# Moving work between engines in a bidirectional RWKV-7 and neighbourhood-attention layer: full-height scores, a transposed inverse, a plain state update

## The chip, the cores and the metric

One core of one Trainium2 chip runs the whole layer in one launch. The metric is device time in microseconds (us), the median of three runs. Engines are named as the profile names them: PE (TensorE matmul) with PEld (its weight loads), DVE (VectorE), ACT (ScalarE), POOL (GpSimd) and SP (SyncE, which issues the DMAs).

## The reference, cut to what matters

The layer normalises 2,560 tokens (2,048 of a prompt, 512 of a sample) of width 1,024, projects them, and runs two groups of heads: 2-D neighbourhood attention, and RWKV-7 in both directions. The change touches the second. Its heart is a recurrence over the tokens, for 8 heads of 64 by 64 states and two directions:

```
def rwkv7_step(S, inp):
    r_t, w_t, k_t, v_t, kk_t, kka_t = inp
    s_kk = jnp.einsum('zbhvk,zbhk->zbhv', S, kk_t)
    S = S * w_t[..., None, :] - s_kk[..., :, None] * kka_t[..., None, :] + v_t[..., :, None] * k_t[..., None, :]
    return S, jnp.einsum('zbhvk,zbhk->zbhv', S, r_t)
```

Around it stand a centred shift of the projected columns, a low-rank product for the decay (`w_up`) and one for the rate (`a_up`), a norm of `kk` for each head, and after it a norm of each head, a bonus and a gate. Both groups of heads then meet in an output projection.

## The kernel before, in words

**Jobs.** The recurrence is done in chunks of 64 tokens. A job is a pair of heads (128 channels), a direction and a block of 512 tokens, so eight chunks. Twenty steps n, each with one job forwards and one backwards, make up the stage: `prep(n+2)`, `inverse(n+1)` and the chain of chunks of step n are written down side by side, with the projection of later heads (`feed`, L921) and, towards the end, the output projection (L1400) beside them.

**`prep`** makes the decays (two low-rank products of two matmuls each, L1124, L1125, L1128, L1129), scales queries and keys with them, and forms for each chunk and head the scores between `A` (128 channels, keys) and `QR` (128 channels, queries): L1172. The two heads lie in channels 0 to 63 and 64 to 127, so each of these products contracts over 64 rows of the array, one head in the upper half, one in the lower. L1175 masks the result into `SC`, L1180 transposes `A`.

**`inverse`** inverts the unit triangular 64 by 64 matrix of each chunk: its 32 by 32 diagonal blocks (32 for each direction, one in each partition) by substitution on DVE, 30 rounds of a product (L1211) and a sum (L1213), and the block beside them by small matmuls (L1232, L1236). The blocks come from `SC` through DRAM (`ad`) and go back through DRAM (`td`).

**`chain_chunk`** is the serial part. For each chunk: a product with the state (L1265) and with the values (L1268), an ACT copy (L1272), a product with the inverse (L1275), an ACT copy (L1276), the outputs (L1279, copied out by L1301) and the state's gain (L1283), and on DVE for each head a new state (state + gain) times the decay, written to another buffer (L1295). The next chunk's L1265 of that direction needs it. The array runs these products as 128 rows by 64 columns, L1265 as 128 by 128.

**What sets the order.** A planner (`Plan.run`) takes all operations with their dependencies, gives each a cost from a formula, and writes out one fixed order for each engine, by the longest tail of work behind an operation; for PE it also weighs the form of the array (128 by 128, 128 by 64, 64 by 128, 32 by 32) against the last one. Buffers are rings of fixed places (`memory`): an operation that takes a place waits for the readers of its last owner. On the chip each engine runs its list in that order, and an instruction that isn't ready holds up all behind it. Instructions of ACT and DVE on one PSUM bank are kept apart by waits too.

## Time and profile before

| | us |
|---|---|
| median of three runs | 2608.29 |
| lowest, highest | 2605.26, 2626.35 |
| the profiled execution | 2613.05 |
| its span (first to last instruction) | 2611.3 |

Of the span PE is busy 91%, DVE 69%, ACT 44%, POOL 36%. PE's mean granted clock is 0.938 of full speed. Busy time of PE counts from an instruction's start to its modelled end, and a busy PE can still be one that waits between instructions. The stage that the change touches lies between about 880 us (first scores) and 2550 us (last chunk); ahead of it come the projections and the attention, behind it the last of the output projection.

### The profile page before, as it was taken

What the parts mean: (1) busy time and instruction counts of PE and PEld (TensorE: products, weight loads), DVE (VectorE), ACT (ScalarE), POOL (GpSimd) and SP (SyncE); (2) the same over time, 40 slices, a digit from 0 to 9 for tenths busy, and PEclk for the clock granted to TensorE, in tenths of its full rate; (3) what the DMA queues carried; (4) which work ended last, traced back from release to release, by engine and by line L of the source; (5) the groups of instructions that cost most, each with busy time, mean ns of one, the idle gap of its engine ahead of it and who ended that gap; (6) DMA issues with size and microseconds to landing.
All of it is one profiled execution on the core that took longest, in us unless ns stands there. A gap on an engine that the chain in (4) does not pass through costs nothing. (4 is left out here: it accounts for less than half of the span.)

```text
span 2611.3 us, 54063 instructions
## 1 busy us (share of the span) xinstructions
PE 2374.5 (91%) x20106; PEld 1667.4 (64%) x20106; DVE 1806.3 (69%) x4932; ACT 1147.2 (44%) x2708; POOL 947.3 (36%) x1079
## 2 busy tenths in 40 slices
PE   6999998988879999989999999998999888999996
PEld 5988997766545555555555665555565666676674
DVE  8873563357656477686887858887778876877435
ACT  7632444466655443444444434444445433433321
POOL 2462662011112453345454434554444433430100
PEclk9999999998889999889999869999899888989998
DMA  7344124277765654355454345454444555445556
GB/s 261 136 150 122 64 66 142 90 212 197 226 184 157 193 160 129 91 152 158 127 141 119 118 124 140 126 168 133 120 135 120 150 155 163 139 132 157 162 172 229
DMA packets 323640, 386.21 MB, mean 148 GB/s; under 512 B 132400, under 2 KB 197808, under 8 KB 321200
## 3 DMA queue, kind: packets, MB, share of 16 engines
q1 hardware_dynamic: 323376, 382.74, 49.3%
q8 instruction: 159, 2.61, 0.4%
q14 instruction: 105, 0.86, 0.1%
HBM read 261.36 MB, written 121.27 MB: 147 GB/s over the span
## 5 line engine op out<-in xcount | busy, mean ns | idle before, releaser
L921 PE MATMUL b<-sbuf 128*128 128x512 f16 x2040 | 578.1, 396 | 19.8 <-DMA sbuf<-xd 13.9
L819 PE MATMUL b<-sbuf 128*128 128x256 f16 x3840 | 454.9, 275 | 15.1 <-ACT sbuf L839 9.1
L819 PEld LDWEIGHTS <-sbuf 128*128 128x128 f16 x3840 | 372.9, 99 | 64.0 <-issue 13.4
L1400 PE MATMUL b<-sbuf 128*128 128x512 f32 x960 | 289.1, 433 | 23.8 <-DVE sbuf L1409 14.3
L921 PEld LDWEIGHTS <-sbuf 128*128 128x128 f16 x2040 | 182.8, 100 | 195.3 <-issue 35.2
L1295 DVE CUSTOM_DVE_ANT_0 sbuf<-b,sbuf 64x64 f32<-64x64 f32 x568 | 160.3, 283 | 167.3 <-ACT sbuf L1301 86.9
L1213 DVE TENSOR_TENSOR sbuf<-sbuf 64x30 f32<-64x30 f32 (+2 forms) x600 | 261.5, 436 | 12.3 <-POOL sbuf L1214 2.5
L1211 DVE TENSOR_TENSOR sbuf<-sbuf 64x30 f32<-64x30 f32 (+2 forms) x600 | 251.7, 420 | 9.9
L1400 PEld LDWEIGHTS b<-sbuf 128*128 128x128 f32 x960 | 179.1, 200 | 71.4 <-DVE sbuf L1409 15.6
L1265 PE MATMUL b<-sbuf 128*128 128x128 f32 x608 | 147.2, 328 | 60.7 <-DVE sbuf L1295 51.4
L1265 PEld LDWEIGHTS b<-sbuf 128*128 128x128 f32 x608 | 103.1, 204 | 126.0 <-issue 41.6
L1272 ACT COPY sbuf<-b 64x128 f32<-64x128 f32 x320 | 81.0, 257 | 215.5 <-PE b L1268 194.5
L1301 ACT COPY sbuf<-b 64x128 f32<-64x128 f32 x320 | 82.7, 262 | 186.5 <-PE b L1283 110.9
L1172 PE MATMUL b<-sbuf 64*128 64x128 f32 x1280 | 156.8, 301 | 4.5 <-POOL sbuf L1162 2.2
L1279 PE MATMUL b<-sbuf 128*64 128x64 f32 x1280 | 151.3, 243 | 6.2 <-ACT sbuf L1276 5.9
L1275 PEld LDWEIGHTS b<-sbuf 128*64 128x64 f32 x1280 | 103.5, 143 | 82.4 <-ACT sbuf L1272 34.4
L1175 DVE TENSOR_TENSOR sbuf<-b,sbuf 128x512 f32<-128x512 f32 x160 | 108.0, 685 | 69.0 <-PE b L1172 46.0
L1279 PEld LDWEIGHTS b<-sbuf 128*64 128x64 f32 x1280 | 105.7, 144 | 77.0 <-ACT sbuf L1276 35.9
L1283 PE MATMUL b<-sbuf 128*64 128x64 f32 x1280 | 154.9, 241 | 0.0
L1017 DVE CUSTOM_DVE_ANT_0 sbuf<-b,sbuf 128x384 f32<-128x384 f32 (+2 forms) x160 | 90.2, 578 | 87.8 <-DMA sbuf<-in_b_top_dram 27.7
L1268 PE MATMUL b<-sbuf 128*64 128x64 f32 x1280 | 150.7, 243 | 0.0
L1275 PE MATMUL b<-sbuf 128*64 128x64 f32 x1280 | 145.6, 240 | 4.6 <-ACT sbuf L1272 4.4
(203 smaller groups left out, 4746.2 us busy)
## 6 DMA issues: line engine op xcount, KB each, us to landing
sbuf<-xd SPq DMA_DIRECT2D x60, 512.0 KB
sbuf<-zrk SPq DMA_DIRECT2D x80, 256.0 KB
sbuf<-zl SPq DMA_DIRECT2D x80, 256.0 KB
sbuf<-in_b_mid_dram SPq DMA_DIRECT2D x32, 512.0 KB
sbuf<-mix SPq DMA_DIRECT2D x28, 448.0 KB
sbuf<-in_x_dram SPq DMA_DIRECT2D x20, 512.0 KB
xd<-sbuf SPq DMA_DIRECT2D x10, 1024.0 KB
sbuf<-qtd SPq DMA_DIRECT2D x40, 256.0 KB
```

The lines of the kernel that those rows point to most:

```text
L819: T.matmul(pa, xx[b][:, k, j * 128:(j + 1) * 128], wt[:, k], start=n == 0, stop=n == 23)
L921: T.matmul(pa, W[wt][:, k], xx[k], start=n == 0, stop=n == 23)
L1172: T.matmul(pa[:, u * 128:(u + 1) * 128], both(A[l0:l0 + 64, u]), both(QR[l0:l0 + 64, u]), start=True, stop=True)
L1211: V.tensor_tensor(out=prod, in0=bc(X[:, i + 1:32, i:i + 1], n, i), in1=bc(X[:, i:i + 1, 0:i], n, i), op=ALU.mult)
L1213: V.tensor_tensor(out=X[:, i + 1:32, 0:i], in0=X[:, i + 1:32, 0:i], in1=prod, op=ALU.add)
L1265: T.matmul(pz[:, 0:128], QR[:, c % 4].rearrange("p a s -> p (a s)"), S0, start=True, stop=False)
L1268: T.matmul(pz[0:64, l0:l0 + 64], SC[:, c % 4, h, 0:64], UV[:, c % 4, l0:l0 + 64], start=S0 is None, stop=S0 is None or h == 1)
L1275: T.matmul(pu[0:64, l0:l0 + 64], SC[:, c % 4, h, 0:64], zs[:, l0:l0 + 64], start=True, stop=True)
L1279: T.matmul(pz[64:128, l0:l0 + 64], SC[:, c % 4, h, 64:128], UV[:, c % 4, l0:l0 + 64], start=S0 is None, stop=S0 is None or h == 1)
L1283: T.matmul(pu[l0:l0 + 64, 128:192], AT[:, c % 4, l0:l0 + 64], UV[:, c % 4, l0:l0 + 64], start=True, stop=True)
L1295: V.tensor_tensor_reduce(out=S1[l, q], in0=src, in1=S0[l, q], scale=gt[l, gcol:gcol + 1], scalar=0.0, op0=ALU.add, op1=ALU.max, accum_out= ...
L1400: T.matmul(pa, m, w, start=j == 0, stop=j == len(todo) - 1)
```

## The change

Four things are changed, in `prep`, `inverse`, `chain_chunk` and one line of `shifted`; the planner and its costs stay.

```diff
@@ prep: scores and the low-rank products over all 128 rows
+    qrz = [tile([128, 4, 128], F32, tag="qrz", name=f"qrz{h}") for h in range(2)]
+    for t in qrz:
+        G.memset(t, 0.0)
...
+            V.tensor_tensor(out=ul[64:128], in0=u[64:128], in1=u[64:128], op=ALU.subtract)
...
-        T.matmul(pw, ul[0:64, 0], lw[0][0:64], start=True, stop=False)
+        T.matmul(pw, ul[:, 0], lw[0], start=True, stop=False)
...
-        T.matmul(pb, ul[0:64, 1], lw[1][0:64], start=True, stop=False)
+        T.matmul(pb, ul[:, 1], lw[1], start=True, stop=False)
...
-        V.tensor_scalar(out=s2[:, :, 1:65], in0=s2[:, :, 1:65], scalar1=1.0, scalar2=None, op0=ALU.add)
+        S.activation(out=s2[:, :, 1:65], in_=s2[:, :, 1:65], func=AF.Copy, bias=1.0)
...
+            for h in range(2):
+                S.copy(out=qrz[h][64 * h:64 * h + 64], in_=QR[64 * h:64 * h + 64].rearrange("p c a s -> p c (a s)"))
             for u in range(4):
-                for l0, pa in zip((0, 64), pas):
-                    T.matmul(pa[:, u * 128:(u + 1) * 128], both(A[l0:l0 + 64, u]), both(QR[l0:l0 + 64, u]),
-                             start=True, stop=True)
+                for z, pa in zip(qrz, pas):
+                    T.matmul(pa[:, u * 128:(u + 1) * 128], both(A[:, u]), z[:, u], start=True, stop=True)
@@ shifted
-                V.tensor_copy(dst[:, :, ::-1] if d else dst, pq[0:2].rearrange("p (c s) -> p c s", s=64))
+                S.copy(out=dst[:, :, ::-1] if d else dst, in_=pq[0:2].rearrange("p (c s) -> p c s", s=64))
@@ inverse
-        X, mt = X[0:64], X[64:128]
-        D.dma_start(mt.rearrange("p s t -> p (s t)"), ad)
+        M, X = X[0:64], X[64:128]
+        D.dma_start(M.rearrange("p s t -> p (s t)"), ad)
...
-        V.reciprocal(rm, rm)
-        V.tensor_copy(rs, rm)
-        V.tensor_scalar(out=rm, in0=rm, scalar1=-1.0, scalar2=None, op0=ALU.mult)
+        V.reciprocal(rs, rm)
+        V.tensor_scalar(out=rm, in0=rs, scalar1=-1.0, scalar2=None, op0=ALU.mult)
...
-        V.tensor_tensor(out=X, in0=mt.rearrange("p s t -> p t s"), in1=bc(rm[:, :, None], 32, 32), op=ALU.mult)
+        V.tensor_tensor(out=M, in0=M, in1=bc(rm[:, None, :], 32, 32), op=ALU.mult)
         for i in range(1, 31):
             n = 31 - i
-            prod = tmp[:, 0:n * i].rearrange("p (s t) -> p s t", t=i)
-            V.tensor_tensor(out=prod, in0=bc(X[:, i + 1:32, i:i + 1], n, i),
-                            in1=bc(X[:, i:i + 1, 0:i], n, i), op=ALU.mult)
-            V.tensor_tensor(out=X[:, i + 1:32, 0:i], in0=X[:, i + 1:32, 0:i], in1=prod, op=ALU.add)
+            prod = tmp[:, 0:n * i].rearrange("p (s t) -> p s t", t=n)
+            V.tensor_tensor(out=prod, in0=bc(M[:, 0:i, i:i + 1], i, n), in1=bc(M[:, i:i + 1, i + 1:32], i, n), op=ALU.mult)
+            V.tensor_tensor(out=M[:, 0:i, i + 1:32], in0=M[:, 0:i, i + 1:32], in1=prod, op=ALU.add)
-        V.tensor_tensor(out=mt.rearrange("p s t -> p t s"), in0=X, in1=bc(rs[:, None, :], 32, 32), op=ALU.mult)
-        G.tensor_tensor(out=X, in0=X, in1=bc(rs[:, None, :], 32, 32), op=ALU.mult)
+        V.tensor_tensor(out=M, in0=M, in1=bc(rs[:, :, None], 32, 32), op=ALU.mult)
+        S.copy(out=X.rearrange("p t s -> p s t"), in_=M)
@@ chain_chunk: one buffer for the state, its decay ahead of the sum
         if d == 1 and S0 is not None and c == 7:
-            s = next_state(d)
-            for l, q in halves:
-                V.tensor_scalar(out=s[l, q], in0=S0[l, q], scalar1=gt[l, 7:8], scalar2=None, op0=ALU.mult)
-            S0 = s
+            S.activation(out=S0, in_=S0, func=AF.Copy, scale=gt[:, 7:8])
...
+        if S0 is not None and scale:
+            S.activation(out=S0, in_=S0, func=AF.Copy, scale=gt[:, gcol:gcol + 1])
...
-                junk = tile([128, 1], F32, tag="junk", name="junk")
-                V.tensor_tensor_reduce(out=S1[l, q], in0=src, in1=S0[l, q], scale=gt[l, gcol:gcol + 1], scalar=0.0,
-                                       op0=ALU.add, op1=ALU.max, accum_out=junk[l])
+                V.scalar_tensor_tensor(out=S1[l, q], in0=src, scalar=by, in1=S0[l, q], op0=ALU.mult, op1=ALU.add)
```

In `memory` the two padded buffers `qrz` take room: QR has 11 places where it had 12, AT 9 where it had 10. Counted over the written orders, VectorE loses the 568 pairs of L1295 for 568 plain operations, 40 operations of L1132, 40 of L962, 24 of L1259, 20 of L1203, and gains 8 (the zeros of `ul`); POOL loses the 20 of L1216; ScalarE gains 160 copies of 64x512, 40 operations of 128x512, 40 of 2x512, 20 copies of 64x1024 and 296 scalings of 128x128. PE has as many instructions as before. With its products sorted by the form of the array (128 rows by 128 columns, 64 by 128, 128 by 64, 32 by 32), PE's order from the stage's first score on changes form 1,828 times before and 1,456 times now.

The planner then writes other orders. On PE, where scores stand in the middle of the stage, before (L1172 scores, L1275 to L1283 the chain's 64-column products, L1180 transposes, L921 the projection of later heads, L1232 and its twin the 32x32 products):

```order
L921 MATMUL b_13650<-sbuf 128x512
L1275 MATMUL b_13625<-sbuf 64x64 x2
L1279 MATMUL b_13616<-sbuf 64x64 x2
L1283 MATMUL b_13616<-sbuf 64x64 x2
L1172 MATMUL b_13639<-sbuf 128x128
L1172 MATMUL b_13699<-sbuf 128x128 x4
L1279 MATMUL b_13625<-sbuf 64x64 x2
L1283 MATMUL b_13625<-sbuf 64x64 x2
L1180 MATMUL b_13711<-sbuf 128x128 x4
```

and now (L1175 scores, L1269, L1273 and L1277 the chain's, L1182 transposes, L1259 the product with the state):

```order
L1273 MATMUL b_14639<-sbuf 64x64 x2
L1277 MATMUL b_14639<-sbuf 64x64 x2
L1175 MATMUL b_14757<-sbuf 128x128 x4
L1175 MATMUL b_14769<-sbuf 128x128 x4
L1262 MATMUL b_14569<-sbuf 64x64 x2
L921 LDWEIGHTS sbuf
L921 MATMUL b_14663<-sbuf 128x512
```

The scores now come head by head, four and four, and in 67 of 135 runs four stand alone.

On ACT inside the chain, before (L1272 and L1276 the chain's two copies, L1301 the output's):

```order
L1276 COPY sbuf<-b_19765 64x128
L1137 ACTIVATE sbuf<-sbuf 128x520
L1138 ACTIVATE sbuf<-sbuf 128x520
L1241 COPY sbuf<-b_19800 32x8x32 x2
L1301 COPY sbuf<-b_19765 64x128
L1272 COPY sbuf<-b_19842 64x128
```

and now (L1266, L1270 and L1294 those three, L1281 the scaling of the state, L1172 the copies into `qrz`):

```order
L1281 ACTIVATE sbuf<-sbuf 128x128
L1172 COPY sbuf<-sbuf 64x512
L1266 COPY sbuf<-b_20443 64x128
L1172 COPY sbuf<-sbuf 64x512
L924 ACTIVATE sbuf<-b_20031,sbuf 128x4x8x16
L1270 COPY sbuf<-b_20443 64x128
L1172 COPY sbuf<-sbuf 64x512 x2
L1281 ACTIVATE sbuf<-sbuf 128x128
L1294 COPY sbuf<-b_20443 64x128
```

The scaling stands directly ahead of the chain's first copy in 91 of 320 cases, and copies into `qrz` stand between the chain's copies.

On DVE at a state update, before (L1295 with its second instruction, L1211 and L1213 the inverse):

```order
L1211 TENSOR_TENSOR sbuf<-sbuf 64x240
L1295 ISA sbuf<-b_18636,sbuf 64x64
L1295 ISA sbuf 64x1
L1213 TENSOR_TENSOR sbuf<-sbuf 64x16x15
L1295 ISA sbuf<-b_18636,sbuf 64x64
L1295 ISA sbuf 64x1
```

and now (L1289 the update, L1213 and L1214 the inverse):

```order
L1213 TENSOR_TENSOR sbuf<-sbuf 64x240
L1289 SCALAR_TENSOR_TENSOR sbuf<-b_18693,sbuf 64x64
L1214 TENSOR_TENSOR sbuf<-sbuf 64x15x16
L1289 SCALAR_TENSOR_TENSOR sbuf<-b_18693,sbuf 64x64
```

An update still has operations of the inverse between its two halves; the second instruction is gone.

## Rows read from the trace of the kernel before

**Rows 1.** The page's busy shares (part 1) and its slices of the span (part 2, 40 slices of 65.3 us; PEclk is the granted clock of PE in tenths of full speed).

```profile
PE 2374.5 (91%) x20106; PEld 1667.4 (64%) x20106; DVE 1806.3 (69%) x4932; ACT 1147.2 (44%) x2708; POOL 947.3 (36%) x1079
...
PEclk9999999998889999889999869999899888989998
```

**Rows 2.** Busy time by stretch, from the first preparation of a job to the last chunk of the recurrence: the stretch in us, its length, busy us and instructions of each engine, granted clock, DMA share, GB/s.

```profile
core 0: us, PE busy (x) PEld busy (x) DVE busy (x) ACT busy (x) POOL busy (x), PEclk, DMA share, GB/s
...
880.00:2550.00 1670.00, 1548.51 (x12645) 1012.41 (x12646) 1239.51 (x3409) 687.20 (x1720) 666.85 (x834) 0.93 0.49 141
```

**Rows 3.** Who waited for whom in the same stretch: us in total, times, longest.

```profile
DVE sbuf L1295 <- ACT sbuf L1301: 86.9, 120, 4.2
...
PE b L1265 <- DVE sbuf L1295: 51.4, 79, 3.1
...
PEld b L1180 <- DVE sbuf L1175: 20.8, 32, 1.6
```

**Rows 4.** TensorE's groups by line (whole span): operation, shapes, count | busy us, mean ns of one | idle before it and what ended it.

```profile
L1400 PE MATMUL b<-sbuf 128*128 128x512 f32 x960 | 289.1, 433 | 23.8 <-DVE sbuf L1409 14.3 <-DVE sbuf L1427 3.9 <-DVE sbuf L1392 1.4
...
L1172 PE MATMUL b<-sbuf 64*128 64x128 f32 x1280 | 156.8, 301 | 4.5 <-POOL sbuf L1162 2.2 <-DVE sbuf L1175 1.7 <-ACT sbuf L1181 0.5
...
L1125 PE MATMUL b<-sbuf 128*128 128x512 f32 x40 | 20.0, 499 | 0.0
...
L1124 PE MATMUL b<-sbuf 64*128 64x512 f32 x40 | 19.7, 492 | 0.0
...
L1128 PE MATMUL b<-sbuf 64*128 64x512 f32 x40 | 18.6, 466 | 0.0
...
L1129 PE MATMUL b<-sbuf 128*128 128x512 f32 x40 | 18.4, 461 | 0.0
```

**Rows 5.** TensorE's instructions in order of time around two blocks of scores (L1172): start us, us from the first start to the last end, then the instructions merged. An fp32 product is two entries here, one for each pass.

```profile
1705.70 0.60 PE L921 MATMUL b<-sbuf 128*128 128x512 f16 x2
1706.24 1.71 PE L1172 MATMUL b<-sbuf 64*128 64x128 f32 x16
1707.88 0.27 PE L1279 MATMUL b<-sbuf 128*64 128x64 f32 x1
...
1708.25 0.49 PE L1265 MATMUL b<-sbuf 128*128 128x128 f32 x2
1708.58 0.38 PE L921 MATMUL b<-sbuf 128*128 128x512 f16 x1
...
1709.15 0.39 PE L921 MATMUL b<-sbuf 128*128 128x512 f16 x1
1709.37 0.60 PE L1180 MATMUL b<-sbuf 128*128 128x128 f32 x4
...
1712.61 1.16 PE L1172 MATMUL b<-sbuf 64*128 64x128 f32 x16
```

**Rows 6.** VectorE's and GpSimd's groups that the change touches, and near ones (columns as in Rows 4).

```profile
L1295 DVE CUSTOM_DVE_ANT_0 sbuf<-b,sbuf 64x64 f32<-64x64 f32 x568 | 160.3, 283 | 167.3 <-ACT sbuf L1301 86.9 <-PE b L1283 32.7 <-ACT sbuf L1276 16.1
...
L1207 DVE TENSOR_TENSOR sbuf<-sbuf 64x1024 f32<-64x1024 f32 x20 | 42.8, 2140 | 30.4 <-DMA sbuf<-ad 26.5 <-POOL sbuf L1156 2.2 <-DMA sbuf<-vtok 1.4
...
L1215 DVE TENSOR_TENSOR sbuf<-sbuf 64x1024 f32<-64x1024 f32 x20 | 39.2, 1959 | 0.6
...
L1216 POOL TENSOR_TENSOR sbuf<-sbuf 64x1024 f32<-64x1024 f32 x20 | 48.4, 2419 | 110.9 <-DVE sbuf L1215 105.4 <-DMA zrk<-sbuf 5.6
...
L1295 DVE DVE_READ_ACCUMULATOR2_ANT sbuf<- 64x1 f32 x568 | 44.7, 79 | 0.1
...
L962 DVE COPY sbuf<-b 2x512 f32<-2x512 f32 x40 | 26.5, 675 | 5.3 <-PE b L959 4.9
...
L848 DVE TENSOR_TENSOR sbuf<-sbuf 128x1024 f32<-128x1024 f32 x20 | 24.8, 1240 | 0.7
...
L1132 DVE TENSOR_SCALAR sbuf<-sbuf 128x512 f32<-128x512 f32 x40 | 22.1, 552 | 12.7 <-ACT sbuf L1126 12.5
...
L1298 DVE TENSOR_TENSOR sbuf<-b,sbuf 64x64 f32<-64x64 f32 x40 | 8.8, 220 | 2.8 <-PE b L1268 1.1 <-ACT sbuf L1301 0.5 <-PE b L1283 0.5
...
L1259 DVE TENSOR_SCALAR sbuf<-sbuf 64x64 f32<-64x64 f32 x24 | 8.1, 338 | 0.4
```

**Rows 7.** ScalarE's groups that are nearest to the added copies and scalings (columns as in Rows 4).

```profile
L1272 ACT COPY sbuf<-b 64x128 f32<-64x128 f32 x320 | 81.0, 257 | 215.5 <-PE b L1268 194.5 <-PE b L1279 13.0 <-PE b L1275 3.2
...
L1152 ACT ACTIVATE sbuf<-sbuf 128x256 f32<-128x256 f32 x80 | 40.0, 507 | 56.4 <-PE b L1265 48.8 <-DMA sbuf<-zrk 4.3 <-POOL sbuf L935 2.6
...
L852 ACT CAST sbuf<-sbuf 128x1024 f16<-128x1024 f32 x20 | 21.0, 1050 | 22.0 <-POOL sbuf L850 10.4 <-DVE sbuf L848 8.8 <-PE b L860 2.8
...
L1330 ACT ACTIVATE sbuf<-sbuf 128x512 f32<-128x512 f32 x20 | 12.6, 629 | 22.8 <-DVE sbuf L1328 10.3 <-POOL sbuf L1328 9.6 <-POOL sbuf L927 1.5
```

**Rows 8.** Busy time in stretches that ran at half the granted clock (columns as in Rows 2): the first and the last of five that follow on a block of scores (the five make 20.4 us), and between them the longest of the stage.

```profile
885.30:892.10 6.80, 6.35 (x22) 4.17 (x22) 3.37 (x4) 1.69 (x3) 3.57 (x6) 0.50 0.39 119
...
1516.70:1564.50 47.80, 47.65 (x267) 30.87 (x268) 26.05 (x78) 14.73 (x37) 10.19 (x20) 0.50 0.33 99
...
2199.40:2202.80 3.40, 3.15 (x18) 2.30 (x18) 2.97 (x5) 0.94 (x1) 0.00 (x0) 0.50 0.92 270
```

**Rows 9.** The scores alone (L1172) in the 5 us ahead of the first and the last of those five: stretch, length, PE busy, PEld busy, granted clock, DMA share, GB/s.

```profile
880.30:885.30 5.00, 1.90 (x16) 1.59 (x16) 1.00 0.44 131
...
2194.40:2199.40 5.00, 1.95 (x13) 1.37 (x12) 1.00 0.99 326
```

More of the change, by code (lines that the diff above doesn't have):

```diff
@@ L581, in memory @@
               *[(t, 32, 1) for t in ("gm", "g8", "rsrg", "rstg")], *[(t, 64, 2) for t in ("ssq", "rsrn", "rstn")])
-    end = max(end, lay(at, ("rs", 128, 2), ("gt", 32, 6), ("junk", 32, 4),
+    end = max(end, lay(at, ("rs", 256, 1), ("gt", 32, 6),
                        *[(t, 32, 2) for t in ("mean", "var", "rsrf", "rstf")]))
@@ L607, in memory @@
         ("rt", 2 * KB, 2), ("kt", 2 * KB, 2), ("smt", 2080, 1), ("s2", 2080, 1), ("Em", 2080, 1), ("E", 2080, 1),
-        ("tha", 2 * KB, 1), ("AK", 2 * KB, 2), ("mkt", KB, 1), ("st", 512, 4), ("rkb", 512, 2),
+        ("tha", 2 * KB, 1), ("AK", 2 * KB, 2), ("mkt", KB, 1), ("st", 512, 2), ("rkb", 512, 2),
         ("QR", 2 * KB, 5), ("bs", 2 * KB, 1), ("tmp", KB, 1), ("zs0", 512, 2), ("zs1", 512, 2))
@@ L612, in memory @@
     lay(X, ("xx", 4 * KB, 4), ("wrh", 2 * KB, 2), ("wrl", 2 * KB, 2), ("UV", 2 * KB, 6), ("yt", 2 * KB, 3),
-        ("QR", 2 * KB, 6), ("AT", 2 * KB, 5), ("SC", 4 * KB, 3), ("rd", 4 * KB, 1))
+        ("QR", 2 * KB, 5), ("AT", 2 * KB, 4), ("SC", 4 * KB, 3), ("qrz", 2 * KB, 2), ("rd", 4 * KB, 1))
     lay(A, ("wl", 2 * KB, 4), ("ml", 2 * KB, 4))
@@ L1080, in encoder_layer @@
     G.memset(s2[:, :, 0:1], 0.0)
-    sts = [[], []]
-    for d in range(2):
-        for i in range(2):
-            t = tile([128, 128], F32, tag="st", name=f"st{d}_{i}")
-            G.memset(t, 0.0)
-            sts[d].append(t)
-    turn = [0, 0]
+    sts = [tile([128, 128], F32, tag="st", name=f"st{d}") for d in range(2)]
+    for t in sts:
+        G.memset(t, 0.0)
     zss, zturn = [[tile([128, 128], F32, tag=f"zs{d}", name=f"zs{d}") for _ in range(2)] for d in range(2)], [0, 0]
@@ L1099, in encoder_layer @@
             steps.append((p, (i, 3 - i)))
+    qrz = [tile([128, 4, 128], F32, tag="qrz", name=f"qrz{h}") for h in range(2)]
+    for t in qrz:
+        G.memset(t, 0.0)
     lora, ydone, state, rkb = {}, set(), {}, {}
@@ L1194, in inverse @@
         X = tile([128, 32, 32], F32, tag="X", name="X")
-        X, mt = X[0:64], X[64:128]
-        D.dma_start(mt.rearrange("p s t -> p (s t)"), ad)
-        rs = tile([128, 32], F32, tag="rs", name="rs")
-        rs, rm = rs[0:64], rs[64:128]
+        M, X = X[0:64], X[64:128]
+        D.dma_start(M.rearrange("p s t -> p (s t)"), ad)
+        rs = tile([64, 2, 32], F32, tag="rs", name="rs")
+        rm, rs = rs[:, 0], rs[:, 1]
         for d, J in enumerate(jobs):
@@ L1244, in inverse @@
                 D.dma_start(UV[64:128], src[:, 4 * i:4 * i + 4])
-    def next_state(d):
-        turn[d] = (turn[d] + 1) % 2
-        return sts[d][turn[d]]
     def chain_chunk(J, c, yt):
@@ L1283, in chain_chunk @@
             T.matmul(pu[l0:l0 + 64, 128:192], AT[:, c % 4, l0:l0 + 64], UV[:, c % 4, l0:l0 + 64], start=True, stop=True)
-        S1 = next_state(d)
+        S1 = sts[d]
         scale = not (d == 1 and last_of_job)
+        if S0 is not None and scale:
+            S.activation(out=S0, in_=S0, func=AF.Copy, scale=gt[:, gcol:gcol + 1])
         for l, q in halves:
-            src = pu[l, 128:192]
-            if S0 is None:
-                if scale:
-                    V.tensor_scalar(out=S1[l, q], in0=src, scalar1=gt[l, gcol:gcol + 1], scalar2=None, op0=ALU.mult)
-                else:
-                    V.tensor_copy(S1[l, q], src)
+            src, by = pu[l, 128:192], gt[l, gcol:gcol + 1]
+            if S0 is None and scale:
+                V.tensor_scalar(out=S1[l, q], in0=src, scalar1=by, scalar2=None, op0=ALU.mult)
+            elif S0 is None:
+                V.tensor_copy(S1[l, q], src)
             elif scale:
-                junk = tile([128, 1], F32, tag="junk", name="junk")
-                V.tensor_tensor_reduce(out=S1[l, q], in0=src, in1=S0[l, q], scale=gt[l, gcol:gcol + 1], scalar=0.0,
-                                       op0=ALU.add, op1=ALU.max, accum_out=junk[l])
+                V.scalar_tensor_tensor(out=S1[l, q], in0=src, scalar=by, in1=S0[l, q], op0=ALU.mult, op1=ALU.add)
             else:
```

4 lines of the change are left out of this document (2 added, 2 removed).

## The prediction, on record before the result was known

> **What bounds the kernel now.** I read the page's shares first, then the stretch that the change touches, then who waits for whom in it, then PE's groups and its order of time, last the other engines' groups. In the stage of 1670 us from 880 to 2550 us PE is busy for 1549, DVE for 1240, ACT for 687, POOL for 667, and PE ran at 0.93 of its clock [rows 2]. The reader should see PE first: nearly always busy, while its longest named idle time is that before L1265, the product with the state, for which DVE's state update L1295 came late, 51.4 us in 79 waits [rows 3]. So the stage is PE's queue with gaps that DVE makes, not a chain with a free PE. What shortens PE's own list, or makes DVE less late, shortens the stage; what only unloads POOL does not; what loads ACT costs nothing as long as ACT's copies are not late.
>
> **The change part by part**, against the profiled execution of 2613.05 us (span 2611.3), which stands 4.8 us above the median of 2608.29.
>
> *Forms of the array.* Two L921 in 0.60 us, of 0.39 each, are 0.21 us apart; after the second, which began at about 1705.92, the first half-height score began at 1706.24, so 0.32 later, 0.1 more [rows 5]. Sixteen passes took 1.71 us; with 0.30 us for one [rows 4] the last began at 1707.65, and the next product came 0.23 later, against 0.11 from a full-height L1265 to an L921, and an ordinary 0.22 from L921 to the full-height transposes L1180 [rows 5]. A change of form costs 0.1 us, then. The orders change form 1,828 times before and 1,456 now, 372 fewer. The 160 matmuls of the low-rank products take 20.0 + 19.7 + 18.6 + 18.4 = 76.7 us, 0.48 each, where L1400, of the same width in one form throughout, takes 289.1 / 960 = 0.30 [rows 4]: in one form they cost 48, so 29 us go, with some 160 of the 372 changes in them. The other 212 make 21. Together **-50 us**.
>
> *Scores.* The two heads' half-height products partly overlap: a block of sixteen passes takes 1.71 us in one place and 1.16 in another [rows 5]; over the stage 156.8 us for 80 blocks are 1.96 each, the half clock among it [rows 4]. At full height they can't overlap: with the transposes' spacing, (0.60 - 0.30) / 3 = 0.10 [rows 5], up to 0.11, sixteen passes take 15 x 0.11 + 0.30 = 1.95. Against 1.96 that costs nothing, against 1.71 it costs 80 x 0.24 = 19, against 1.16 it costs 80 x 0.79 = 63. I take **+15**, near the ordinary block; ends 0 and 63. The Trainium skill (TensorE: Matmul & The Clock Gate, Part 3) says that matmuls on different row groups of the array run concurrently, and so speaks against full height: by it every block would have been like the short one, and the sum would be worse by 48 us. The trace agrees with it in some blocks only.
>
> *DVE.* The second instruction of L1295 goes, 44.7 us; L962 and L1132 go to ACT, 26.5 and 22.1, L1259 too, 8.1. L1207 and L1215, which read or wrote the matrix against its rows at 2140 and 1959 ns, become operations on rows; L848, of as many elements in a partition, takes 1240: 82.0 - 2 x 24.8 = 32. The rounds of the inverse keep their sizes (outer and inner length change places), so I cost them at nothing. The new update adds a sum and a scalar to one PSUM operand, between L1298 at 220 and L1295 at 283 ns; I take 283. All of it is 134 us less of 1806 [rows 6]. It lies beside PE's work; what counts is how late DVE is for PE. Of 51.4 + 20.8 us of such waits [rows 3] I take **-25**: half of the first, since two of the things that stand between an update's halves go or shorten; ends 0 and -72.
>
> *POOL.* L1216, 20 x 2.4 us, becomes a copy on ACT of about L852's 1.05 us [rows 6, 7]. It lies between one inverse and the next, with DMAs on both sides, and I cost it at nothing; were the inverse the bound, it would be 27 us less.
>
> *ACT.* 160 copies into `qrz` and 80 operations that come from DVE at L1330's 629 ns are 151 us; 296 scalings of 128x128 lie between L1272's 257 and L1152's 507 ns, I take 0.35: 104; the 20 copies of the inverse make 21 [rows 7]. ACT goes from 1147 [rows 1] to some 1420 us, 54% of the span, and is nowhere full. But queued behind a scaling or a `qrz` copy are the chain's copies, and PE waits for those; scores now wait for ACT too, and there is one pair of `qrz`. Half of the 160 `qrz` copies 0.1 us late are **+8**; the ends are 0 (every copy lies in idle time) and +104 (every scaling delays the chain; a rival). QR and AT lose a place; a job's second direction then waits for the chain of two steps ago, as SC, with ten places throughout, makes it do already: nothing.
>
> *Clock.* Of the half-clock stretches, five of together 20.4 us follow on scores [rows 8, 9]; 20.4 us at half clock cost 10. Full-height scores keep twice the array at work, and I take **-10**; ends -30, if stretches with scores in them like that of 47.8 us [rows 8] also end sooner, and +20, if thinner PE work elsewhere brings new ones.
>
> Sum: -50 + 15 - 25 + 8 - 10 = -62, so 2551 us, and with the 4.8 us **2546 us** on the median's scale.
>
> **The rivals.**
>
> *A, the forecast:* PE's queue is the bound, 2546, with its own range from 2500 to 2590: chance 0.55.
>
> *B, DVE is the bound:* the inverse of 60 operations a step keeps DVE the critical queue, and all of its 134 us come off: 2613 - 134 - 5 = 2474. For it speaks that L1265 waits for DVE and for little else; against it that DVE is busy 74% of the stage and PE 93% [rows 2]. Chance 0.13.
>
> *C, nothing much:* the gaps that DVE leaves are made by the order, not by its load, the clock stays, scores lose 19 and ACT's lateness takes 20: 2613 - 50 + 19 + 20 - 5 = 2597, within 1%. For it: the mean block of scores hides a loss only because of the half clock in it. Chance 0.17.
>
> *D, slower: ACT stands in the chain.* A scaling becomes ready with L1265, just ahead of L1268, so it is put ahead of the chain's first copy. If each of 296 holds the chain up by its 0.35 us, and the chain sets the end, 104 us are added to -50 + 15: 2613 + 69 - 5 = 2677. It turns slower than 1% at (26 + 35) / 296 = 0.21 us of delay for each. For it: DVE waits for L1301 on ACT for 86.9 us already [rows 3]. Against it: ACT sat idle 215.5 / 320 = 0.67 us ahead of each first copy [rows 7], room for a scaling. Chance 0.09.
>
> *E, the rule of row groups holds throughout:* all blocks overlapped, and 63 us are lost against 50 won, with nothing from DVE: 2613 + 13 - 5 = 2621. The Trainium skill's section named above would have it so. The mean of 1.96 us a block [rows 4] speaks against. Chance 0.06.
>
> **How the numbers follow.** A measurement of this kernel tells 1%, 26 us, from no change: faster is below 2582, slower above 2634. A gives 0.53 of its 0.55 to faster, B all; C splits 0.03 to faster and 0.14 to same; D gives 0.08 to slower, E 0.02. That makes faster 0.69, same 0.21, slower 0.10. The range that leaves 2 in 10 out reaches from between B and A, 2480, to E, 2622: it leaves out half of B, D and the end of E. The wide bounds (DVE 0 to -72, scores 0 to 63) are within it.
>
> **What would show each step.** Changes of form: score entries should begin 0.22 us after an L921, low-rank matmuls should take 0.3. Scores: sixteen passes at 1.9 us at full clock. DVE: busy near 1670, no second instruction, updates at 220 to 283 ns, L1207's and L1215's successors at 1.2 us. ACT: near 1420, scalings at 0.3 to 0.4. PE before the product with the state: idle for 25 us on DVE, not 51. Clock: above 0.94. I would be wrong if rounds of the inverse took another time in the new layout, if PE waited for ACT's copies by tens of us, or if PE's busy time fell and the span did not.

## The result and the profile after

| | before | after |
|---|---|---|
| median on one chip, us | 2608.65 | 2510.97 |
| lowest, highest | 2605.26, 2626.35 | 2500.88, 2514.51 |
| profiled execution | 2613.05 | 2511.51 |
| its span | 2611.3 | 2509.7 |

The ratio is 0.9606, with an interval from 0.9555 to 0.9657. The change takes off 98 us where I forecast 62; the time is within the range and on the forecast's side, 35 us below its number. Three executions in a slower state are left out of every median, mean and ratio here: one of 3433 us (clock 0.585) of same_order_half, one of 2625 us of lag_before, one of 2640 us of the kernel before.

First the page's shares and its clock line, then the cores' clock, of the kernel after:

```profile
PE 2298.2 (92%) x20106; PEld 1652.1 (66%) x20106; DVE 1697.4 (68%) x4248; ACT 1418.1 (57%) x3264; POOL 870.8 (35%) x1059
...
PEclk9999999998999999999999999999999899999998
```

```profile
core 0: 2509.7 us, clock 0.965
```

The same answer for the kernel before:

```profile
core 0: 2611.3 us, clock 0.938
```

The granted clock of TensorE has two levels here, full (2.4 GHz) and half (1.2 GHz). So a mean of c over a span s holds 2 x (1 - c) x s at half: 324 us before, 176 after. Work that goes at half clock would take half that time at full, so the 148 us less are worth up to 74 of the 101.6 us by which the two spans differ. That is the first reading to make: most of the gain stands beside the clock, for which I had forecast 10.

The record has span and clock of every execution, not only of the profiled one. A span times its clock is, by the same estimate, what it would take at full clock all the way. Over 25 executions of the kernel before (in the sessions of the experiments) spans from 2589 to 2627 us give 2446 to 2461, 2452 on the mean; four of the kernel after give 2420 to 2428, 2423 on the mean. So executions of one kernel differ mostly by their clock, and of the 98 us between the mean spans (2606 and 2508) 69 are clock and 30 the rest.

The stage of the recurrence, from the first scores to the last chunk (columns as in [rows 2]):

```profile
880.00:2451.00 1571.00, 1469.91 (x12654) 994.69 (x12652) 1145.54 (x2757) 955.57 (x2275) 592.07 (x816) 0.97 0.52 150
```

It is 99 us shorter than in [rows 2]; PE's busy time fell by 79 and its idle time from 121 to 101. Who waits for whom in it, PE first (line, what it waited for: us, times, longest):

```profile
PE b L1259 <- DVE sbuf L1289: 25.6, 61, 1.3
PE b L1273 <- ACT sbuf L1270: 12.9, 22, 1.8
PE b L1269 <- ACT sbuf L1266: 9.5, 19, 1.4
...
PE b L1259 <- ACT sbuf L1294: 6.1, 12, 1.1
```

L1259 is the product with the state (L1265 before), L1289 the new update (L1295 before). The 51.4 us of [rows 3] have halved. The next rows are new in size: PE's waits for ACT's copies in the chain, 28.5 us together. Before they were 12.5:

```profile
PE b L1279 <- ACT sbuf L1276: 5.9, 13, 1.3
PE b L1275 <- ACT sbuf L1272: 4.4, 11, 0.9
...
PE b L1265 <- ACT sbuf L1301: 2.2, 2, 2.1
```

So half of DVE's lateness went, and 16 us of waits came back as ACT's. The groups that answer to [rows 4, 6, 7], of the kernel after:

```profile
L1213 DVE TENSOR_TENSOR sbuf<-sbuf 64x30 f32<-64x30 f32 (+2 forms) x600 | 252.0, 420 | 11.2
L1214 DVE TENSOR_TENSOR sbuf<-sbuf 64x30 f32<-64x30 f32 (+2 forms) x600 | 247.9, 413 | 11.9
L1289 DVE SCALAR_TENSOR_TENSOR sbuf<-b,sbuf 64x64 f32<-64x64 f32 x568 | 160.2, 282 | 163.9 <-ACT sbuf L1294 97.6 <-PE b L1277 44.9 <-PE b L1269 2.8
...
L1209 DVE TENSOR_TENSOR sbuf<-sbuf 64x1024 f32<-64x1024 f32 x20 | 26.5, 1325 | 42.2 <-DMA sbuf<-ad 42.1
L1216 DVE TENSOR_TENSOR sbuf<-sbuf 64x1024 f32<-64x1024 f32 x20 | 26.1, 1304 | 0.3
```

```profile
L1281 ACT ACTIVATE sbuf<-sbuf 128x128 f32<-128x128 f32 x284 | 113.1, 402 | 94.2 <-PE b L1259 91.7
L1172 ACT COPY sbuf<-sbuf 64x512 f32<-64x512 f32 x160 | 98.7, 617 | 50.2 <-PE b L1175 33.1 <-POOL sbuf L1163 7.8 <-POOL sbuf L1160 3.8
...
L1266 ACT COPY sbuf<-b 64x128 f32<-64x128 f32 x320 | 80.8, 257 | 52.0 <-PE b L1262 47.2 <-PE b L1273 1.4
L1217 ACT COPY sbuf<-sbuf 64x1024 f32<-64x1024 f32 x20 | 39.7, 1985 | 5.3 <-DVE sbuf L1216 5.0
```

```profile
L1125 PE MATMUL b<-sbuf 128*128 128x512 f32 x40 | 20.4, 510 | 4.0 <-DVE sbuf L1177 3.7 <-DMA sbuf<-vtok 0.3
L1129 PE MATMUL b<-sbuf 128*128 128x512 f32 x40 | 20.0, 500 | 0.4 <-ACT sbuf L1183 0.4
L1130 PE MATMUL b<-sbuf 128*128 128x512 f32 x40 | 16.8, 421 | 0.0
L1126 PE MATMUL b<-sbuf 128*128 128x512 f32 x40 | 15.9, 399 | 0.0
```

The update is one instruction of 282 ns instead of two. The two big products of the inverse went from 2140 and 1959 ns to 1325 and 1304. ACT's idle time ahead of the chain's first copy (L1266) fell from 215.5 us [rows 7] to 52: the scalings L1281 and the copies L1172 lie in it. The four low-rank groups add up to 73.1 us, where they were 76.7 [rows 4]; the sum of durations thus shows 4 us for a step to which I gave 29. The experiments tell what it is worth.

### The profile page after: what moved, and what is told of

It is laid out like the page before. It is cut to its first block, busy times and chain, and to the rows that moved or that the text cites. A ratio compares the mean times of both kernels' runs of the same rounds, so it can differ in the third digit from the quotient of the medians.

```text
span 2509.7 us, 53916 instructions
## 1 busy us (share of the span) xinstructions
PE 2298.2 (92%) x20106; PEld 1652.1 (66%) x20106; DVE 1697.4 (68%) x4248; ACT 1418.1 (57%) x3264; POOL 870.8 (35%) x1059
## 4 chain that ended last, share of the span: by engine, by line
PE 58%; DVE 15%; DMA 14%; ACT 8%; issue 4%; SPq 1%; POOL 1%; DVEq 0%; ACTq 0%; POOLq 0%
PE b L819 15%; PE b L921 11%; PE b L1393 6%; PE b L1175 5%; DVE sbuf L1213 3%; DVE sbuf L1214 3%; DVE sbuf L1289 3%; PE b L1259 3%; PE b L1269 2%; PE b L1262 2%; DMA sbuf<-vad 2%; PE b L1273 2%; PE b L1023 2%; DMA sbuf<-td 1%; DMA sbuf<-xd 1%
## 5 line engine op out<-in xcount | busy, mean ns | idle before, releaser
L921 PE MATMUL b<-sbuf 128*128 128x512 f16 x2040 | 562.6, 387 | 14.6 <-DMA sbuf<-xd 9.4
L819 PEld LDWEIGHTS <-sbuf 128*128 128x128 f16 x3840 | 374.9, 99 | 64.8 <-issue 12.5
L921 PEld LDWEIGHTS <-sbuf 128*128 128x128 f16 x2040 | 177.9, 99 | 179.2 <-issue 22.8
L1289 DVE SCALAR_TENSOR_TENSOR sbuf<-b,sbuf 64x64 f32<-64x64 f32 x568 | 160.2, 282 | 163.9 <-ACT sbuf L1294 97.6
L1213 DVE TENSOR_TENSOR sbuf<-sbuf 64x30 f32<-64x30 f32 (+2 forms) x600 | 252.0, 420 | 11.2
L1214 DVE TENSOR_TENSOR sbuf<-sbuf 64x30 f32<-64x30 f32 (+2 forms) x600 | 247.9, 413 | 11.9
L1393 PEld LDWEIGHTS b<-sbuf 128*128 128x128 f32 x960 | 175.9, 196 | 66.6 <-DVE sbuf L1402 15.5
L1175 PE MATMUL b<-sbuf 128*128 128x128 f32 x1280 | 178.4, 288 | 2.8 <-DVE sbuf L1177 1.2
L1259 PE MATMUL b<-sbuf 128*128 128x128 f32 x608 | 140.8, 315 | 43.7 <-DVE sbuf L1289 25.6
L1175 PEld LDWEIGHTS b<-sbuf 128*128 128x128 f32 x1280 | 163.9, 200 | 16.4 <-issue 4.9
L1259 PEld LDWEIGHTS b<-sbuf 128*128 128x128 f32 x608 | 96.9, 194 | 111.3 <-DVE sbuf L1289 25.3
L1281 ACT ACTIVATE sbuf<-sbuf 128x128 f32<-128x128 f32 x284 | 113.1, 402 | 94.2 <-PE b L1259 91.7
L1273 PEld LDWEIGHTS b<-sbuf 128*64 128x64 f32 x1280 | 100.1, 137 | 85.0 <-ACT sbuf L1270 46.3
L1273 PE MATMUL b<-sbuf 128*64 128x64 f32 x1280 | 143.3, 235 | 13.8 <-ACT sbuf L1270 12.9
L1244 POOL MEMSET sbuf<- 64x512 f32 x80 | 41.1, 518 | 328.0 <-PE b L1277 197.4
L1277 PE MATMUL b<-sbuf 128*64 128x64 f32 x1280 | 152.4, 233 | 0.0
L1269 PE MATMUL b<-sbuf 128*64 128x64 f32 x1280 | 140.3, 235 | 10.0 <-ACT sbuf L1266 9.5
L1269 PEld LDWEIGHTS b<-sbuf 128*64 128x64 f32 x1280 | 100.2, 139 | 74.5 <-ACT sbuf L1266 42.5
L1294 ACT COPY sbuf<-b 64x128 f32<-64x128 f32 x320 | 83.6, 263 | 110.6 <-PE b L1277 57.5
```

What stands on the lines that cost most here:

```text
L819: T.matmul(pa, xx[b][:, k, j * 128:(j + 1) * 128], wt[:, k], start=n == 0, stop=n == 23)
L921: T.matmul(pa, W[wt][:, k], xx[k], start=n == 0, stop=n == 23)
L1175: T.matmul(pa[:, u * 128:(u + 1) * 128], both(A[:, u]), z[:, u], start=True, stop=True)
L1213: V.tensor_tensor(out=prod, in0=bc(M[:, 0:i, i:i + 1], i, n), in1=bc(M[:, i:i + 1, i + 1:32], i, n), op=ALU.mult)
L1214: V.tensor_tensor(out=M[:, 0:i, i + 1:32], in0=M[:, 0:i, i + 1:32], in1=prod, op=ALU.add)
L1259: T.matmul(pz[:, 0:128], QR[:, c % 4].rearrange("p a s -> p (a s)"), S0, start=True, stop=False)
```

## The experiments

**The theories.** K (the clock): products on half of the array's rows keep TensorE longer at half clock; the height of the scores alone makes a good part of the gain. Against it stand: the gain is the relief of DVE, and the clock only follows shorter gaps; it is PE's shorter list (changes of form); or it is the luck of another order that the planner wrote out.

All twelve runs in one table. Ratios are against the kernel before on the same chip in the same session, whose median was 2604 in the first four runs, 2614 in the next four, 2600 in the last; the kernel after stands at 0.9606. They are the ratios on record; those of three of the second four (same_order_half, same_order_lora, lag_after) lie 0.4 to 0.6% above the quotients of the medians, so medians and ratios are to be compared each with their own kind. Span and clock are of each profiled execution, the half-clock time is 2 x (1 - clock) x span (to some 3 us), and "of it clock" is half of what it stands above the 176 us of the kernel after. The last two columns are such differences from the kernel after on the means of all executions (25 of the kernel before, nine of lag_before, four of each other): what the clock costs, and the span at full clock. Single executions of a kernel scatter by some 10 us in the first and 4 in the second (standard deviation).

| run | median us | ratio | span | clock | at half clock | span above after | of it clock | mean: clock | mean: rest |
|---|---|---|---|---|---|---|---|---|---|
| before | 2608.65 | 1 | 2611.3 | 0.938 | 324 | 101.6 | 74 | 69 | 30 |
| half_scores | 2552.84 | 0.9778 | 2550.9 | 0.949 | 260 | 41.2 | 42 | 38 | 2 |
| only_full | 2563.69 | 0.9823 | 2566.7 | 0.954 | 236 | 57.0 | 30 | 33 | 21 |
| old_update | 2526.37 | 0.9687 | 2528.8 | 0.961 | 197 | 19.1 | 11 | 9 | 7 |
| old_inverse | 2522.67 | 0.9679 | 2523.1 | 0.966 | 172 | 13.4 | -2 | 4 | 10 |
| same_order_half | 2548.44 | 0.9810 | 2534.6 | 0.956 | 223 | 24.9 | 24 | 43 | -6 |
| same_order_lora | 2526.27 | 0.9710 | 2521.9 | 0.964 | 182 | 12.2 | 3 | 9 | 9 |
| lag_after | 2508.77 | 0.9641 | 2515.1 | 0.963 | 186 | 5.4 | 5 | 4 | -4 |
| lag_before | 2605.34 | 0.9980 | 2599.8 | 0.945 | 286 | 90.1 | 55 | 66 | 31 |
| dve_back | 2528.08 | 0.9714 | 2531.1 | 0.956 | 223 | 21.4 | 24 | 23 | -5 |
| no_scale | 2491.87 | 0.9583 | 2501.1 | 0.966 | 170 | -8.6 | -3 | -11 | -4 |
| pool_scale | 2547.49 | 0.9792 | 2548.5 | 0.956 | 224 | 38.8 | 24 | 34 | 6 |
| no_qrz | 2503.92 | 0.9619 | 2503.5 | 0.966 | 170 | -6.2 | -3 | 2 | -8 |

**1. The scores alone back to half height** (half_scores: the kernel after without `qrz`; the planner writes its own order for it).

```diff
-                for z, pa in zip(qrz, pas):
-                    T.matmul(pa[:, u * 128:(u + 1) * 128], both(A[:, u]), z[:, u], start=True, stop=True)
+                for l0, pa in zip((0, 64), pas):
+                    T.matmul(pa[:, u * 128:(u + 1) * 128], both(A[l0:l0 + 64, u]), both(QR[l0:l0 + 64, u]),
+                             start=True, stop=True)
```

> The changed kernel with the scores at half height again (no qrz copies, QR and AT with their old places), all else changed. Theory K, that scores over all rows hold PE's clock: the half-clock time between 880 us and the chain's end goes from 89 us back towards the 229 us before, at least to 150, and the time rises from 2511 to between 2540 and 2570. Rival D, that the lighter DVE takes the gaps away and the clock follows the gaps: half-clock time stays under 110 us and the time between 2490 and 2515, since copies on ACT go too.

2552.84 us, 42 above the kernel after, and the span's difference of 41 is all clock by the table (38 of 40 on the means). The half-clock time of the stage is 167 us, in K's band. What follows: the scores' height makes some two fifths of the gain. Its order differs too, though, so this alone does not separate height from order.

**2. Full height alone, on the kernel before** (only_full: scores and low-rank products over 128 rows; update, inverse and engines as before).

```diff
+            V.tensor_tensor(out=ul[64:128], in0=u[64:128], in1=u[64:128], op=ALU.subtract)
...
-        T.matmul(pw, ul[0:64, 0], lw[0][0:64], start=True, stop=False)
+        T.matmul(pw, ul[:, 0], lw[0], start=True, stop=False)
...
-                for l0, pa in zip((0, 64), pas):
-                    T.matmul(pa[:, u * 128:(u + 1) * 128], both(A[l0:l0 + 64, u]), both(QR[l0:l0 + 64, u]),
-                             start=True, stop=True)
+                for z, pa in zip(qrz, pas):
+                    T.matmul(pa[:, u * 128:(u + 1) * 128], both(A[:, u]), z[:, u], start=True, stop=True)
```

> The kernel before with the full-height scores and low-rank products alone (with the qrz copies on ACT and the new places of QR and AT), inverse, state update and DVE copies as before. Theory K: the half-clock time of the stage falls from 229 us to under 130 and the time from 2609 to between 2535 and 2565. Rival D: half-clock time stays above 180 us and the time between 2585 and 2610; PE's waits for DVE before the product with the state stay at 45 us or more in both.

The ratio 0.9823 is 46 us. The span is 44.6 below the kernel before and the half-clock time 88 less, which is 44; on the means of all executions full height takes 36 us of clock off the kernel before (117 against 153) and 9 of the rest. The time is where K put it; the half-clock time of the stage, 154 us, lies between the two bands. Half of the whole gain, then, is to be had by height alone with DVE as late as before (49 us of PE's waits are still for the update), and the rest needs the other parts.

**3 and 4. The old update and the old inverse in the kernel after.** old_update brings back two buffers a direction and

```diff
-                V.scalar_tensor_tensor(out=S1[l, q], in0=src, scalar=by, in1=S0[l, q], op0=ALU.mult, op1=ALU.add)
+                V.tensor_tensor_reduce(out=S1[l, q], in0=src, in1=S0[l, q], scale=gt[l, gcol:gcol + 1], scalar=0.0,
+                                       op0=ALU.add, op1=ALU.max, accum_out=junk[l])
```

without the scalings on ACT; old_inverse brings back `X` and `mt` with their products against the rows and POOL's product, as before.

> The changed kernel with the old state update on DVE (two buffers, two instructions for each head, no scalings on ACT). Theory K: half-clock time of the stage stays under 120 us; the time is 2511 plus at most 20, or a little less, since 113 us of scalings leave ACT. Rival D: PE's wait for the state update goes from 26 us back to 40 or more, half-clock time to 130 us or more, and the time to between 2530 and 2560.

> The changed kernel with the old inverse (columns, the two transposing operations at 2 us on DVE, the last product on POOL). Theory K: half-clock time of the stage stays under 120 us and the time within 15 us of 2511. Rival D: the two 2 us operations make DVE late, PE's waits for DVE grow by 15 us or more and the time goes to between 2530 and 2550.

15 and 12 us slower by the medians, both in K's bands; the intervals of their ratios (from 0.9654 and from 0.9636) still touch that of the kernel after (to 0.9657). PE's wait for the update grows from 25.6 to 37.4 and 32.3 us. The old inverse costs its time with little clock (0.966 in the profiled execution; 4 us against 10 of the rest on the means), and half of that rest is the longer wait. Of the old update's 19 us of span the clock makes 11 (9 of 16 on the means).

**5. The kernel after's very order, each score on its own 64 rows** (same_order_half). The planner is given the full-height product, and the operands are cut after it has counted its cost and form.

```diff
-                for z, pa in zip(qrz, pas):
-                    T.matmul(pa[:, u * 128:(u + 1) * 128], both(A[:, u]), z[:, u], start=True, stop=True)
+                for l0, z, pa in zip((0, 64), qrz, pas):
+                    op = T.matmul(pa[:, u * 128:(u + 1) * 128], both(A[:, u]), z[:, u], start=True, stop=True)
+                    op.args = (op.args[0], both(A[l0:l0 + 64, u]), z[l0:l0 + 64, u])
```

> The changed kernel, planned as it is, so with the very same order on every engine, the same qrz copies and waits; only when it is written out does each score product take the 64 rows of its head (the other rows of qrz are zeros, so the result is the same). Theory K, that the height of the products itself holds the clock: half-clock time of the stage rises from 89 us to 150 or more and the time by 25 to 45 us, to 2536 to 2556. Rival O, that the gain comes from the order which the planner writes for full-height products: half-clock time stays under 115 us, and the time within 12 us of 2511 (changes of form come back for some 20 us, overlap of the two heads takes as much off).

Nothing differs but the rows that these 1,280 entries use, and the median is 37 us higher, the ratio 2.1% (0.981, from 0.9751 to 0.9869, against 0.9606, to 0.9657). The profiled execution was its quickest, 24.9 us of span above the kernel after; its half-clock time is 47 us more, so 24 us, all of it. In the stage it is 147 us, just under K's band and far above O's.

```profile
core 0: 2534.6 us, clock 0.956
```

All four executions together say more: they ran at 0.946 to 0.956, those of the kernel after at 0.963 to 0.969. On the means the span is 38 us longer, with 43 us of clock and 6 less of the rest. This is the run that settles K's core, that the height of the scores moves the clock: order, ACT's copies, DVE and the planned waits are the same. Two views of it show both halves of what height does. First, what the array does in one place in full clock, in order of time; the kernel after, then same_order_half:

```profile
898.56 0.81 PE L921 MATMUL b<-sbuf 128*128 128x512 f16 x3
899.21 1.95 PE L1175 MATMUL b<-sbuf 128*128 128x128 f32 x16
900.99 0.38 PE L921 MATMUL b<-sbuf 128*128 128x512 f16 x1
```

```profile
895.08 0.81 PE L921 MATMUL b<-sbuf 128*128 128x512 f16 x3
895.82 1.71 PE L1175 MATMUL b<-sbuf 64*128 64x128 f32 x16
897.46 0.39 PE L921 MATMUL b<-sbuf 128*128 128x512 f16 x1
```

From the first L921 to the one behind the scores it is 2.43 us at full height and 2.38 at half. Half height wins 0.24 by overlap and pays 0.19 at its two ends. By this block height is worth next to nothing on PE's own list: 0.05 x 80 = 4 us against full height, near the 6 us of the means. Second, the stretches at half clock. In the kernel after, two that hold a whole block of scores (columns as in [rows 2]; then the scores alone in them):

```profile
1331.70:1338.50 6.80, 6.80 (x41) 5.59 (x37) 5.44 (x14) 2.67 (x6) 0.98 (x1) 0.50 0.39 116
1966.60:1973.40 6.80, 6.77 (x40) 6.27 (x40) 5.68 (x9) 3.60 (x10) 6.80 (x7) 0.50 0.24 80
...
1331.70:1338.50 6.80, 3.62 (x16) 3.53 (x16) 0.50 0.39 116
1966.60:1973.40 6.80, 3.69 (x16) 3.61 (x16) 0.50 0.24 80
```

In same_order_half, the 5 us before its longest one, that stretch, and the scores in it:

```profile
1976.20:1981.20 5.00, 3.11 (x35) 2.34 (x34) 4.64 (x12) 4.62 (x12) 3.77 (x6) 1.00 0.07 27
...
1981.20:2008.50 27.30, 26.12 (x147) 20.91 (x147) 20.23 (x45) 13.59 (x36) 10.49 (x10) 0.50 0.57 167
...
1981.20:2008.50 27.30, 8.29 (x32) 7.11 (x32) 0.50 0.57 167
```

And the scores in the longest one of the kernel before, the 47.8 us of [rows 8]:

```profile
1516.70:1564.50 47.80, 8.60 (x32) 6.83 (x32) 0.50 0.33 99
```

PE stood idle for 1.9 of the 5 us before the clock fell, with no score in them; then it was busy for 26 of 27.3 us and stayed at half, with two blocks of half-height scores in that time, as in the 47.8 us of the kernel before. The two stretches of the kernel after were over after 6.8 us. So I read it that half-height scores don't so much bring the half clock as keep it: the stage has about as many half-clock stretches in both (16, and 15 in the kernel after), but 147 us in them against 89.

That reading is not shown. Six of the 16, together 51 us, also have scores in the 5 us ahead of them; in the kernel after it is one, of 3.4 us. And full height is no guard: stretches with full-height scores in them lasted 10.2 us in the kernel after, 23.9 us in only_full and 34.1 us in pool_scale (run 11). The last of these, whole and then its scores alone:

```profile
2050.90:2085.00 34.10, 28.40 (x234) 23.01 (x234) 18.86 (x53) 18.32 (x39) 18.19 (x24) 0.50 0.60 158
...
2050.90:2085.00 34.10, 3.99 (x16) 3.61 (x16) 0.50 0.60 158
```

Shown is that the height of the scores moves the half-clock time; how it does so stays open.

**6. The low-rank products likewise** (same_order_lora): the order kept, the first product of each pair on 64 rows again.

```diff
+        op.args = (op.args[0], ul[0:64, 0], lw[0][0:64])
```

(and the same for the second pair)

> The same with the low-rank products instead of the scores: planned as in the changed kernel, written out with 64 rows for the two first products of each pair. By the prediction's term of 29 us for them the time rises by 20 to 30 us, to 2531 to 2541; if the term was too large, since in the changed kernel's trace these 160 matmuls still take 73 us of busy time against 77, by under 12 us.

15 us by the medians, 12 by the profiled spans, of which the clock makes 3; on the means 18, of which 9 are clock. The time lies between the two bands. By durations the step was worth 76.7 - 73.1 = 4 us, so the gain does not lie in what these rows add up.

**7 and 8. Another order of the same work.** One constant of the planner, in the kernel after and in the kernel before.

```diff
-LAG = 20.0
+LAG = 19.0
```

> The changed kernel with the planner's LAG at 19 instead of 20: another order of the same work, to see how much the time depends on chance in the order. Theories K and D both expect 2511 plus or minus 10, half-clock time of the stage 75 to 110 us. A rival, that the change drew a lucky order, expects a time of 2530 or more.

> The kernel before with LAG at 19: another order of its work. Theories K and D expect 2609 plus or minus 12 and half-clock time of the stage over 190 us. The rival, that the kernel before had an unlucky order, expects under 2585 and half-clock time under 160 us.

2508.77 and 2605.34: neither moved (0.9641 against 0.9606, with overlapping intervals; 0.9980 of before, from 0.9936 to 1.0023). One other order of each kernel shows no luck of an order. The row of lag_before also shows how far single executions scatter: a median within 3 us of before, and a profiled execution with 11.5 us less span and 38 us less at half clock.

**9. Two operations back on DVE** (dve_back: the add of 1 and the copies of the norms).

```diff
-        S.activation(out=s2[:, :, 1:65], in_=s2[:, :, 1:65], func=AF.Copy, bias=1.0)
+        V.tensor_scalar(out=s2[:, :, 1:65], in0=s2[:, :, 1:65], scalar1=1.0, scalar2=None, op0=ALU.add)
...
-                S.copy(out=dst[:, :, ::-1] if d else dst, in_=pq[0:2].rearrange("p (c s) -> p c s", s=64))
+                V.tensor_copy(dst[:, :, ::-1] if d else dst, pq[0:2].rearrange("p (c s) -> p c s", s=64))
```

> The changed kernel with two of the moves to ACT undone: the addition of 1 (40 of 128x512) and the copies of the norms (40 of 2x512) are DVE's again. DVE gets 48 us back, ACT loses 47. If moving work from DVE to ACT is worth something by itself, the time rises by 8 to 20 us from 2511; if PE is indifferent to where these lie (they are in preparation, not in the chain), it stays within 6 us.

17 us for 46 us more of DVE (1743.5 us busy), in the band for moves that are worth something by themselves. PE's waits for the update, and the clock:

```profile
PE b L1259 <- DVE sbuf L1289: 34.8, 62, 2.4
```

```profile
core 0: 2531.1 us, clock 0.956
```

No product on the array changed here, and the half-clock time still rose by 47 us; but no stretch of its stage lasts longer than 10.2 us, there are more of them (22, against 15). On the means all of the cost is clock (23 us, the rest 5 less). So something besides height moves the clock, and K is not the whole of it. That it is DVE's gaps fits, but isn't shown: the planner wrote another order here, and old_inverse, with 71 us more of DVE work (1768.4 us busy) and nearly the same wait for the update (32.3 us), has only 4 us of clock.

**10 and 11. ACT's share: scalings left out, and moved to POOL.**

```diff
-        if S0 is not None and scale:
-            S.activation(out=S0, in_=S0, func=AF.Copy, scale=gt[:, gcol:gcol + 1])
```

```diff
-            S.activation(out=S0, in_=S0, func=AF.Copy, scale=gt[:, gcol:gcol + 1])
+            G.tensor_scalar(out=S0, in0=S0, scalar1=gt[:, gcol:gcol + 1], scalar2=None, op0=ALU.mult)
```

> The changed kernel without the scaling of the state by its decay ahead of the sum (284 ACT operations left out, so the state is not the reference's). The price of ACT in the chain: by the forecast's term the scalings cost next to nothing, and the time is 2500 to 2513; by rival D at least 0.1 us each, and the time falls by 28 us or more, to under 2483.

> The changed kernel with those 284 scalings on POOL, which has the most room (35% busy), instead of ACT. If ACT's lateness is what costs, the time falls by 10 us or more, to under 2501. If it costs nothing, the time is 2505 to 2530, since POOL is slower for each and holds up DVE where both work in SBUF.

Without the scalings 19 us less by the medians, 6 by the ratios, whose intervals overlap (0.9529 to 0.9637): at the most 19 / 284 = 0.07 us for each. The time lies between the two bands. On POOL the kernel is 36 us slower, which no theory had. Its scalings, and what DVE's update then waits for:

```profile
L1281 POOL TENSOR_SCALAR sbuf<-sbuf 128x128 f32<-128x128 f32 x284 | 227.4, 801 | 447.3 <-PE b L1259 440.5 <-ACT sbuf L1127 5.9
```

```profile
DVE sbuf L1289 <- ACT sbuf L1294: 131.4, 146, 6.8
```

They take 801 ns, twice as long as on ACT, and the update waits 131 us where it waited 97.6. PE's waits for the update grew by only 5 us. Of the 38.8 us of span the clock makes 24; on the means it makes 34 of 40, so the cost is mostly clock. Why the clock falls with POOL's scalings, under another order of the same products, stays open.

**12. The copies into `qrz` left out** (no_qrz: scores against the zeros that stand there).

```diff
-            for h in range(2):
-                S.copy(out=qrz[h][64 * h:64 * h + 64], in_=QR[64 * h:64 * h + 64].rearrange("p c a s -> p c (a s)"))
```

> The changed kernel without the 160 copies into qrz (the scores are taken against zeros, so the result is not the reference's). The price of the copies: by the forecast's term of 8 us the time is 2498 to 2511; if scores wait for them in PE's order, it falls by 20 us or more, to under 2491. The half-clock time of the stage stays under 110 us by theory K, since the products keep their height.

2503.92 us, in the band of the forecast's term and 7 less by the medians, while the ratio 0.9619 is that of the kernel after: 98.7 us of copies on ACT cost little or nothing that can be measured.

Of the versions that leave nothing out, none was clearly quicker than the kernel after.

## Why the prediction was right, and where its sum was not

Direction, range and the bound were right: A, PE's queue, with B, C, D and E refuted. B needed DVE to be the critical queue; but only_full, with DVE as busy as before (1805 us), wins half of the gain, and old_inverse, with 71 us more of DVE work, loses 12. C needed the clock to stay. D needed 0.21 us a scaling; no_scale leaves 0.07 at most. The sum came out right in sign for partly wrong reasons: the terms outside the clock were put at -52, the clock at -10, and the profiled spans show about -28 and -74, the means -30 and -69. That two misses of opposite sign left the total within the range is in part luck.

**Forms of the array and scores, -50 + 15.** The mechanism is as read: a form change costs 0.1 us. In the two timelines above the scores begin 0.31 us after the last L921 at half height, 0.22 at full. (Of the forecast's own two gaps the second was 0.20 us, not 0.23, since the last entry began at 1707.68; the 0.1 stands.) The Trainium skill (TensorEngine Tiling (Array Packing), Tiling Modes, Key Properties) says that changing the tiling mode drains TensorE; these rows show a later start, which agrees, and no drain as such. Sixteen full-height passes take 1.95 us, as forecast. The two nearly cancel, as -21 + 15 had it: measured 4 us the other way, or 6 on the means. The low-rank step was over-sized: 9 us outside the clock and 18 with it, not 29. I had priced it by durations (0.48 against 0.30 us each), and the four products still last 0.40 to 0.51 at full height; the row of one width that I compared them with did not carry over. Rival E's rule (the Trainium skill, TensorE: Matmul & The Clock Gate, Part 3: products on different row groups run concurrently) is borne out by the 0.24 us that overlap wins, but here the 0.19 at the block's two ends take four fifths of it back.

**DVE, -25.** The wait fell from 51.4 to 25.6 us, as said. By the profiled executions the parts of this step are worth 15 (old_inverse) and 8 (old_update) us outside the clock, so 23; by the means 10 and 7. DVE's busy time is 25 us above my 1672; the two products at 1325 and 1304 ns instead of 1240 explain 3 of that. I had added up durations, and durations on DVE overlap: they add up to 2018 us before and 1859 after, 159 less, where busy time, which counts an overlap once, fell by 109. The rounds kept their times (420 and 413 ns against 420 and 436). **POOL, 0**: PE's waits for `td` stayed at a few us.

**ACT, +8.** Busy 1418 against 1420, the scalings 0.40 against 0.35 us, the strided copy L1217 1.99 against 1.05. PE's waits for ACT's copies rose by 16, twice the term; on the means no_scale and no_qrz are 4 and 8 us shorter outside the clock, of the term's size and at the edge of what can be told apart.

**Clock, -10: the step that failed, in size.** It said "five of together 20.4 us follow on scores", and priced those alone, with -30 as its end. The count was short: two more stretches of the kernel before, 17.1 us at 1366.5 and 6.8 us at 2097.0, have scores (6 and 12 entries) in the 5 us ahead of them, so it is seven of together 44.4 us. And it left out stretches that have scores in them and none ahead, like those of 47.8 and 27.3 us. The end of -30 names that case ("if stretches with scores in them like that of 47.8 us also end sooner"), and gave it too little. It also put the clock's answer to the other parts at nothing. Measured, the term is -74 by the profiled spans and -69 by the means.

Four kernels split it, by what the clock costs on the mean of all executions: 153 us in the kernel before, 117 with full height alone (only_full), 123 with the other parts and half-height scores (half_scores, its low-rank products at full height), 85 with both. Height is thus worth 36 to 38 us of clock, 43 in one order (same_order_half), and the other parts 30 to 33. Which of the other parts does it stays open: taken back one by one they cost 4 (old_inverse), 9 (old_update), 9 (same_order_lora) and 23 us of clock (dve_back, in another order).

The account on the means: of 98 us of span, 69 clock; outside the clock inverse 10, low-rank 9, update 7, scores -6, together some 21 of the 30 that are left. The other 9 have no row; with an error of some 2 us in each mean, and the kernel after in all four differences, they may be noise.
